# The modulation product of a two-layer diffusion block moved from TensorE to VectorE, all but its first four groups

## The chip, the cores and the metric

The kernel runs on 1 core of one Trainium2 chip. The metric is the device time of one execution in microseconds (us). The kernel before took 1662.61 us, the median of three runs (1662.46 to 1664.08). All times of rows come from one profiled execution of it, whose span is 1662.0 us.

## The reference, cut to what matters

Two layers (D_MODEL 1024) work on 256 tokens x and 256 tokens of context. Each has a mixer of three branches (spatial gating, differential attention, a gated delta rule) and a feed-forward with a convolution. Both are entered through a norm that is scaled and shifted by the modulation, and left through a gate by it. The modulation is one vector of 6144 numbers per layer for x and one for the context, each a product of a vector of 1024 with a matrix:

```
mod_x = silu(c) @ w_mod[l] + b_mod[l]            # [1, 6144]
mod_c = silu(c_ctx) @ w_mod[l] + b_mod[l]
sh1_x, sc1_x, gt1_x, sh2_x, sc2_x, gt2_x = split(mod_x, 6)
h_x = rms_norm(x, norm1_g[l]) * (1 + sc1_x) + sh1_x
y_x, y_c = hybrid_mixer(h_x, h_c, ...)           # the same for ctx
x = x + gt1_x * y_x
h_x = rms_norm(x, norm2_g[l]) * (1 + sc2_x) + sh2_x
x = x + gt2_x * conv_ffn(h_x, ...)               # silu(gate) * val, w_up, w_down
...
return x
```

The last layer goes on with x alone behind the mixer's inputs: of its modulation the context's half is needed for the first shift and scale only.

## The kernel before, in words

Activations lie with features on partitions and 512 tokens (256 of context, 256 of x) along the row; in the last layer 256 behind the mixer's keys. A projection goes by column tiles of 128 features. For each, SP loads the weights as f32, 512 KB (`wr`, three buffers, L266); ScalarE rounds them to a first part `wh` and VectorE subtracts for the rest `wl` (`split`, L262, four buffers each); TensorE multiplies wh by hh, wl by hh and wh by hl (`mm3`, L284), where hh and hl are the two parts of the activations. A column tile with 1024 inputs is 24 products of 512 columns.

The names of the rows: pqkv, pqk and ptm are projections of the mixer, psc the attention scores, pwo the output projection, pup and pdn the two projections of the feed-forward. In the delta rule sX, sL, sT, sLC and sLR belong to the triangular solve (`gdn_solve`, L1146), a chain of small VectorE operations sT, sL, sT, sL, ... on tiles of 32 x 32; U is its result, and the scan over chunks follows. axc, asq, qkss, qkrs and rsqt belong to the norm of attention's queries and keys.

A norm ends (`norm_end`, L522) with a chain: pss sums the squares, rsqv to rs is an inverse square root in small VectorE operations, pb spreads it over the partitions on TensorE, then xn, hh and hl are made, and the next projection starts with the first of them. TensorE has none of its big products to do meanwhile; three of these gaps bear on the change: ahead of the feed-forward of layer 0, ahead of layer 1, ahead of its feed-forward.

The modulation before (`mod_product`, L449) uses the conditioning as the stationary operand: per half group of 256 columns SP loads 1 MB of w_mod (`wm`), and 8 products of 128 x 32 by 256 columns add into `pmod`. A group (512 features, of 12 per layer) ends with `mod_finish` (L455): a VectorE transpose `m` of 128 x 512, four small products pmc, and one addition of the bias into `modv`. Groups go where the program calls `mod`: four of layer 0 at the start, six in its mixer behind the solve, the last two as filler in the gap ahead of the feed-forward, layer 1's first four inside layer 0's feed-forward, and the rest as filler in the gap ahead of layer 1, in its mixer and in its gap.

The order of the work is set by a list scheduler when the kernel is built: it takes the instructions of the program by priority and its own estimate of times and writes a fixed order for each engine; the delta rule is wrapped in `high_priority`. On the chip each engine then runs its list strictly in turn, SP's list of loads too: a load that waits for its buffer holds all loads behind it.

Of the kernel before, what the change touches and what calls it, by code (L numbers as in the profile page):

```python
# [10 lines left out]
F32 = mybir.dt.float32  # L11
# [16 lines left out]
FILL = (("p4", "p4"), ("t4a", "t4b"))  # L28
# [68 lines left out]
def host_layout(i):  # L97
# [7 lines left out]
    o["wmod"] = f(i["w_mod"].reshape(L, 8, 128, 12, 2, 256).transpose(0, 3, 4, 2, 1, 5))  # L105
# [67 lines left out]
class _Kernel:  # L173
# [97 lines left out]
    def wblock(self, src, n, step):  # L271
        """the two float32r parts of a block of weights [128, n], in pieces of `step` columns."""
# [16 lines left out]
    def proj_fm(self, src, kt, xh, xl, c0, ps):  # L289
        """ps[:, :NT-c0] = W^T x for one column tile of W laid out [128, kt*128]."""  # L290
# [5 lines left out]
    def first_load(self, srcs, i, j):  # L296
        """half i of the rows of column tiles j and j + 1, to be split by first_w."""
# [17 lines left out]
    def proj_first(self, srcs, xh, xl, c0, pss):  # L315
        """as proj_fm for several column tiles at once; goes along with h as its parts appear."""
# [21 lines left out]
    def run(self):  # L338
# [4 lines left out]
        for l in range(L):  # L343
# [3 lines left out]
            early = self.mod(1, (4, 5, 6), (5,), "g") if last else iter(())  # L347
            hh, hl = self.norm_end(N, steps(early, 2, 3, 2) if last else self.first)
            c0 = 256 if last else 0
            xf, N = self.mixer(l, hh, hl, xsrc, c0, early)  # L350
            late = self.mod(l, (10, 11), (), "g")
            hh, hl = self.norm_end(N, steps(late, 2, 3, 1))
            N = self.ffn(l, hh, hl, xf, c0, itertools.chain(late, self.mod(1, range(4), (9, 10)) if not last else ()))
# [11 lines left out]
    def start(self):  # L365
# [18 lines left out]
        for n, loads in enumerate((((0, 0), (0, 2)), ((0, 4),), ((1, 0), (1, 2)), ())):  # L384
            self.mod_ahead(0, order[2 * n:2 * n + 2], places[2 * n:2 * n + 2])
# [10 lines left out]
    def load_rest(self):  # L396
        """the constants and parameters that the first products do without."""
# [33 lines left out]
    def mod_load(self, l, g, h, where):  # L431
        """half of the columns of group g, [128, 8, 256], in a slot or in tiles of a part of its size."""
        src = self.a["wmod"][l, g, h]
        if isinstance(where, int):
# [31 lines left out]
    def mod(self, l, groups, places, tag="a"):  # L466
# [916 lines left out]
```

## Time and profile before

| | before |
|---|---|
| median of 3 runs | 1662.61 us |
| span of the profiled execution | 1662.0 us |
| TensorE busy | 1623.0 us, 98% |
| VectorE busy | 1084.7 us, 65% |
| ScalarE busy | 760.9 us, 46% |
| chain that ends last, through TensorE | 88% |

The profiled execution's own time is known as its span alone; it lies 0.6 us below the median. A busy share is an average over the span: a stage can be bound by an engine that is half idle in the whole. The chain names what released what, back from the last instruction. In a timeline row the bracket says how long the engine was idle before and on whom it waited. Matmuls overlap, so that their starts, not their durations, tell TensorE's pace.

### The profile page before, as it was taken

The numbers are of one execution on the slowest core, as the hardware profiler recorded it, in microseconds if no ns is written. First come the engines' busy times: TensorE is split into PE (matmuls) and PEld (weight loads), VectorE is DVE, ScalarE is ACT, GpSimd is POOL, SyncE is SP. The second block draws the span as 40 slices with busy tenths as digits, with TensorE's granted clock in tenths as the row PEclk, the third lists the DMA queues.
The fourth block names the chain that finished last, engine by engine and source line by source line (L and its number), as shares of the span: only waits on it lengthen the run. The fifth ranks groups of instructions, "written<-read, shape, count | busy, mean of one in ns | idle before, by whom it ended". The sixth has DMA issues, their size and how long they took to land.

```text
span 1662.0 us, 28498 instructions
## 1 busy us (share of the span) xinstructions
PE 1623.0 (98%) x11278; PEld 1355.4 (82%) x11278; DVE 1084.7 (65%) x2557; ACT 760.9 (46%) x1445; POOL 6.6 (0%) x16
## 2 busy tenths in 40 slices
PE   5999999999999999999999999999999999999999
PEld 3777887876788887778888887778878799999999
DVE  5658678666744456756446655658678775788685
ACT  3553622256532333534234442653722764566564
POOL 0000000000000000000000000000000000000000
PEclk9999899999999999999999999999999999999999
DMA  8553111421233444533333335441114356755665
GB/s 327 202 192 118 40 39 52 140 89 39 74 92 102 145 147 155 213 127 93 92 107 101 97 120 169 164 154 52 40 52 140 92 153 224 226 155 174 190 185 153
DMA packets 61254, 217.24 MB, mean 131 GB/s; under 512 B 7104, under 2 KB 13248, under 8 KB 55360
## 3 DMA queue, kind: packets, MB, share of 16 engines
q1 hardware_dynamic: 59248, 207.65, 39.3%
q10 hardware_dynamic: 1872, 7.77, 1.3%
q8 instruction: 88, 1.44, 0.4%
q14 instruction: 46, 0.38, 0.1%
HBM read 212.25 MB, written 3.15 MB: 130 GB/s over the span
## 4 chain that ended last, share of the span: by engine, by line
PE 88%; DVE 5%; ACT 2%; DMA 2%; issue 1%; SPq 0%; ACTq 0%; DVEq 0%
PE pup L239 22%; PE pg L239 11%; PE pdn L239 11%; PE pqkv L239 7%; PE ptm L239 7%; PE pbr L239 6%; PE pwo L239 3%; PE pmod L239 3%; PE pu L239 2%; PE psc L239 2%; PE pS L239 2%; PE pj L239 1%; ACT U L236 1%; PE pkS L239 1%; PE po L239 1%; PE pV L239 1%
## 5 line engine op out<-in xcount | busy, mean ns | idle before, releaser
L236 ACT ACTIVATE wh<-wr 128x512 fp32r<-128x512 f32 (+1 forms) x594 | 367.6, 622 | 441.8 <-PE pdn L239 108.5
L218 DVE TENSOR_TENSOR wl<-wr,wh 128x512 fp32r<-128x512 f32 (+1 forms) x592 | 400.1, 680 | 236.1 <-ACT wh L236 233.3
L239 PE MATMUL pup<-hh,wh 128*128 128x512 f32 (+1 forms) x704 | 237.9, 338 | 1.0 <-ACT hh L236 0.9
L239 PE MATMUL pup<-hh,wl 128*128 128x512 f32 (+1 forms) x704 | 236.8, 337 | 0.0
L239 PE MATMUL pup<-hl,wh 128*128 128x512 f32 (+1 forms) x704 | 236.2, 336 | 0.0
L233 DVE SCALAR_TENSOR_TENSOR fcv<-pup,par,fcv 128x510 f32<-128x510 f32 (+1 forms) x176 | 107.3, 611 | 81.4 <-ACT fcv L236 81.1
L239 PEld LDWEIGHTS pup<-hh,wh 128*128 128x128 f32 x704 | 133.6, 190 | 17.6 <-ACT fcv L236 2.5
L239 PEld LDWEIGHTS pup<-hl,wh 128*128 128x128 f32 x704 | 133.5, 190 | 14.0 <-DVE hl L233 0.2
L239 PEld LDWEIGHTS pup<-hh,wl 128*128 128x128 f32 x704 | 133.7, 190 | 13.6
L239 PE MATMUL ptm<-wh,hh 128*128 128x256 f32 x448 | 132.1, 295 | 0.0
L239 PE MATMUL ptm<-wh,hl 128*128 128x256 f32 x448 | 131.4, 294 | 0.0
L239 PE MATMUL pg<-hh,wl 128*128 128x512 f32 (+1 forms) x384 | 130.8, 341 | 0.0
L239 PE MATMUL pg<-hh,wh 128*128 128x512 f32 (+1 forms) x384 | 130.7, 340 | 0.1
L239 PE MATMUL ptm<-wl,hh 128*128 128x256 f32 x448 | 130.6, 292 | 0.0
L239 PE MATMUL pg<-hl,wh 128*128 128x512 f32 (+1 forms) x384 | 129.9, 338 | 0.0
L239 PE MATMUL pdn<-fh,wh 128*128 128x512 f32 (+1 forms) x352 | 118.5, 337 | 0.0
L239 PE MATMUL pdn<-fh,wl 128*128 128x512 f32 (+1 forms) x352 | 118.3, 336 | 0.0
L239 PE MATMUL pdn<-fl,wh 128*128 128x512 f32 (+1 forms) x352 | 118.0, 336 | 0.0
L236 ACT ACTIVATE fcv<-pup,par 128x512 f32<-128x512 f32 (+1 forms) x88 | 51.1, 581 | 91.1 <-PE pup L239 91.1
L239 PEld LDWEIGHTS ptm<-wh,hh 128*128 128x128 f32 x448 | 88.1, 197 | 4.7 <-issue 4.2
L239 PEld LDWEIGHTS ptm<-wh,hl 128*128 128x128 f32 x448 | 88.2, 197 | 3.3 <-issue 2.9
L239 PEld LDWEIGHTS ptm<-wl,hh 128*128 128x128 f32 x448 | 87.9, 196 | 2.8 <-issue 2.2
(326 smaller groups left out, 3121.9 us busy)
## 6 DMA issues: line engine op xcount, KB each, us to landing
wr<-in_wup_dram SPq DMA_DIRECT2D x80, 512.0 KB, 3.7
wm<-in_wmod_dram SPq DMA_DIRECT2D x39, 1024.0 KB, 7.6
wr<-in_wfm_dram SPq DMA_DIRECT2D x78, 512.0 KB, 3.6
wr<-in_wtm_dram SPq DMA_DIRECT2D x32, 512.0 KB, 3.7
wr<-in_wdn_dram SPq DMA_DIRECT2D x32, 512.0 KB, 3.6
wr<-in_wbr_dram SPq DMA_DIRECT2D x24, 512.0 KB, 3.6
wr<-in_wo_dram SPq DMA_DIRECT2D x16, 512.0 KB, 4.3
wm<-in_wmod_dram SPq DMA_DIRECT2D x14, 512.0 KB, 4.2
```

What stands on the lines that cost most here:

```text
L218: self.nc.vector.tensor_tensor(out=out, in0=a, in1=b, op=op)
L233: self.nc.vector.scalar_tensor_tensor(out=out, in0=a, scalar=s, in1=b, op0=op0, op1=op1)
L236: self.nc.scalar.activation(out, a, f, bias=bias, scale=scale, **k)
L239: self.nc.tensor.matmul(out, lhsT, rhs, start=start, stop=stop, **k)
```

## The change

Four groups of layer 0 stay as they are, at the start. The other 80 column tiles of 128 features (32 of layer 0, 48 of layer 1) come from a transposed copy of w_mod, `wmt`, with a tile's features on partitions and the 1024 inputs along the row. SP loads one such tile (512 KB, one buffer); VectorE multiplies it by silu of the conditioning (`scb`, the same on all partitions, loaded and passed through one ScalarE instruction at the start of the mixer) with one scalar_tensor_tensor whose accum_out is the sum along the row: a feature's product. The context takes one such instruction, its products written to `mj`, and x another, written over the tile. Layer 1's tiles from 16 on are done for x alone. After four tiles one addition adds the bias. The generator `mod` is advanced by `more`, one tile at a time, between column tiles of the projections of layer 0 (70 tiles in the text of the program; the last ten are asked for by `branch` in layer 1). The fillers in the gaps go. The bulk of the rest is deleted comments; gains and gates of the last layer are taken for x alone.

```
 def host_layout(i):
-    o["wmod"] = f(i["w_mod"].reshape(L, 8, 128, 12, 2, 256).transpose(0, 3, 4, 2, 1, 5))
+    o["wmod"] = f(i["w_mod"][0, :, :2048].reshape(8, 128, 4, 2, 256).transpose(2, 3, 1, 0, 4))
+    o["wmt"] = f(np.concatenate([i["w_mod"][0, :, 2048:], i["w_mod"][1]], 1).T.reshape(80, 128, 1024))
+    o["cB"] = f(np.broadcast_to(np.stack([i["c_ctx"], i["c"][0]], 0)[None], (128, 2, 1024)))
...
-            early = self.mod(1, (4, 5, 6), (5,), "g") if last else iter(())
-            hh, hl = self.norm_end(N, steps(early, 2, 3, 2) if last else self.first)
+            hh, hl = self.norm_end(N, iter(()) if last else self.first)
             c0 = 256 if last else 0
-            xf, N = self.mixer(l, hh, hl, xsrc, c0, early)
-            late = self.mod(l, (10, 11), (), "g")
-            hh, hl = self.norm_end(N, steps(late, 2, 3, 1))
-            N = self.ffn(l, hh, hl, xf, c0, itertools.chain(late, self.mod(1, range(4), (9, 10)) if not last else ()))
+            if not last:
+                self.mods = self.mod()
+            xf, N = self.mixer(l, hh, hl, xsrc, c0)
+            hh, hl = self.norm_end(N)
+            N = self.ffn(l, hh, hl, xf, c0)
...
-    def mod_load(self, l, g, h, where):
...
-    def mod(self, l, groups, places, tag="a"):
-        """modv[l] for groups of 4 column tiles, silu(cond) @ w_mod + b_mod; yields after each half of the columns,
-        which go through the next of `places` if they aren't there, and after each group."""
-        at = itertools.cycle(places)
-        for g in groups:
-            pm = None
-            for h in range(2):
-                r = self.wm.pop((g, h), None) or self.mod_load(l, g, h, next(at))
-                if pm is None:
-                    pm = self.bank(tag, "pmod")
-                self.mod_product(pm[:, 256 * h:256 * h + 256], r)
-                yield
-            self.mod_finish(l, pm, 4 * g, 4)
+    def mod(self):
+
+
+        nc = self.nc
+        sb = self.cp.tile([128, 2, 1024], F32, tag="scb", name="scb")
+        nc.sync.dma_start(out=sb, in_=self.a["cB"])
+        self.act(sb, sb, AF.Silu)
+        for n in range(80):
+            l, j = (0, 16 + n) if n < 32 else (1, n - 32)
+            vs = (0, 1) if l == 0 or j < 16 else (1,)
+            w = self.wp.tile([128, 1024], F32, tag="wm", name="wmt", bufs=1)
+            nc.sync.dma_start(out=w, in_=self.a["wmt"][n])
+            if n % 4 == 0:
+                m4 = self.small("m4", [128, 4, 2], bufs=2)
+            for v in vs:
+                o = w if v else self.tmp("mj", [128, 1024], BF16)
+                nc.vector.scalar_tensor_tensor(out=o, in0=w, scalar=1.0, in1=sb[:, v], op0=ALU.mult, op1=ALU.mult,
+                                               accum_out=m4[:, n % 4, v:v + 1])
+            if n % 4 == 3:
+                self.add(self.modv[l][:, j - 3:j + 1, vs[0]:], m4[:, :, vs[0]:],
+                         self.P(l, "bmod", j - 3, 4).unsqueeze(2).to_broadcast([128, 4, len(vs)]))
             yield
+
+    def more(self, n=1):
+        for _ in range(n):
+            next(self.mods, None)
...
-        for _ in itertools.chain(early, self.mod(l, range(4 + 3 * l, 10), ((5, 7, 8, 9), (5, 7, 8))[l])):
-            pass
...
-            if m == 1:
-                self.mod_ahead(l, ((10, 0), (10, 1), (11, 0), (11, 1)), (1, 8) + FILL)
...
 def branch(self, i, y, acc, final):      # behind each column tile of the gate
+            if l > 0 or i == 0 or i == 2 and m < 2:
+                self.more()
...
 def sgu(self):                           # and gdn_z; attn_project once per projection
+            self.more(l == 0)
...
 def ffn(self, l, hh, hl, xf, c0):
-                    next(mods, None)
+                if l == 0:
+                    self.more()
...
-                if m == 2 and hf == 1 and l + 1 < L:
-                    self.mod_ahead(l + 1, ((4, 0), (4, 1), (5, 0), (5, 1), (6, 0)), FILL + (("t4c", "gS"), ("tg",) * 4, ("go", "go", "go", "ta")))
+                if l == 0:
+                    self.more(1 + hf)
...
-            if hf == 0:
-                for _ in mods:
-                    pass
...
-    nc = bacc.Bacc("TRN2", target_bir_lowering=False, num_devices=1)
+    nc = bacc.Bacc("TRN2", target_bir_lowering=False, num_devices=1, dynamic_dma_scratch_size=1024)
```

The scheduler moves the new instructions: all 128 of VectorE stand before layer 1. The first place is VectorE in the solve of layer 0, between the sX transposes and sLR. Before:

```order
L218 TENSOR_TENSOR sT<-sX,sL 128x207
L218 TENSOR_TENSOR sL<-sL,sT 128x23x9
L218 TENSOR_TENSOR sT<-sX,sL 128x220
L218 TENSOR_TENSOR sL<-sL,sT 128x22x10
L218 TENSOR_TENSOR sT<-sX,sL 128x231
L218 TENSOR_TENSOR sL<-sL,sT 128x21x11
L218 TENSOR_TENSOR sT<-sX,sL 128x240
L218 TENSOR_TENSOR sL<-sL,sT 128x20x12
L218 TENSOR_TENSOR sT<-sX,sL 128x247
L218 TENSOR_TENSOR wl<-wr,wh 128x512
L218 TENSOR_TENSOR sL<-sL,sT 128x19x13
```

Now, at the same step of the chain (wmt and mj are the new products, m the sums, rsqt and qkrs the attention norm):

```order
L219 TENSOR_TENSOR wl<-wr,wh 128x512
L219 TENSOR_TENSOR sL<-sL,sT 128x22x10
L234 SCALAR_TENSOR_TENSOR qkrs<-rsqt,qkrs 128x8
L219 TENSOR_TENSOR wl<-wr,wh 128x512
L219 TENSOR_TENSOR sT<-sX,sL 128x231
L219 TENSOR_TENSOR axc<-axc,qkrs 128x512
L219 TENSOR_TENSOR sL<-sL,sT 128x21x11
L219 TENSOR_TENSOR sT<-sX,sL 128x240
L471 SCALAR_TENSOR_TENSOR mj,m_2038<-wmt,scb 128x1024
L219 TENSOR_TENSOR sL<-sL,sT 128x20x12
L471 SCALAR_TENSOR_TENSOR wmt,m_2038<-wmt,scb 128x1024
L219 TENSOR_TENSOR sT<-sX,sL 128x247
```

Two new products stand inside the chain sT, sL, and the attention projection's wl, axc and small operations have moved in among them; from the sX transposes to sLR VectorE has 116 instructions before and 178 now.

The second place is VectorE in the gap ahead of the feed-forward of layer 0, from the last sum of squares to xn. Before:

```order
L458 STREAM_TRANSPOSE m_6254<-pmod 128x512
L230 TENSOR_SCALAR rsqv<-pss 128x4
L230 TENSOR_SCALAR rs<-rsqv 128x4
L218 TENSOR_TENSOR rsqt<-rs 128x4
L218 TENSOR_TENSOR rsqt<-rsqt,rsqv 128x4
L233 SCALAR_TENSOR_TENSOR rsqt<-rsqt 128x4
L218 TENSOR_TENSOR modv_90<-pmc,part 128x8
L233 SCALAR_TENSOR_TENSOR rs<-rsqt,rs 128x4
L458 STREAM_TRANSPOSE m_6324<-pmod 128x512
L218 TENSOR_TENSOR rsqt<-rs 128x4
L233 SCALAR_TENSOR_TENSOR rsqt<-rsqt,rsqv 128x4
L218 TENSOR_TENSOR modv_90<-pmc,part 128x8
```

Now:

```order
L471 SCALAR_TENSOR_TENSOR mj,m_6385<-wmt,scb 128x1024
L231 TENSOR_SCALAR rsqv<-pss 128x4
L471 SCALAR_TENSOR_TENSOR wmt,m_6385<-wmt,scb 128x1024
L231 TENSOR_SCALAR rs<-rsqv 128x4
L219 TENSOR_TENSOR rsqt<-rs 128x4
L219 TENSOR_TENSOR rsqt<-rsqt,rsqv 128x4
L234 SCALAR_TENSOR_TENSOR rsqt<-rsqt 128x4
L234 SCALAR_TENSOR_TENSOR rs<-rsqt,rs 128x4
L219 TENSOR_TENSOR rsqt<-rs 128x4
L234 SCALAR_TENSOR_TENSOR rsqt<-rsqt,rsqv 128x4
L234 SCALAR_TENSOR_TENSOR rs<-rsqt,rs 128x4
```

Both transposes and both additions into modv are gone; one new product stands in front of rsqv and one between rsqv and rs.

The third place is SP's queue. Before, in layer 0, from the end of the first down projection through the second half of the feed-forward (x22) into the second down projection:

```order
L268 DMA wr<-in_wdn_dram 128x384
L268 DMA wr<-in_wup_dram 128x1024 x22
L268 DMA wr<-in_wdn_dram 128x1024
L268 DMA wr<-in_wdn_dram 128x384
L268 DMA wr<-in_wdn_dram 128x1024
L268 DMA wr<-in_wdn_dram 128x384
L268 DMA wr<-in_wdn_dram 128x1024
L442 DMA wm_8831<-in_wmod_dram 128x512
```

Now, where the second half of the feed-forward passes into its down projection:

```order
L466 DMA wmt<-in_wmt_dram 128x1024
L269 DMA wr<-in_wdn_dram 128x1024
L466 DMA wmt<-in_wmt_dram 128x1024
L269 DMA wr<-in_wdn_dram 128x384
L466 DMA wmt<-in_wmt_dram 128x1024
L269 DMA wr<-in_wdn_dram 128x1024
L466 DMA wmt<-in_wmt_dram 128x1024
L269 DMA wr<-in_wdn_dram 128x384
L466 DMA wmt<-in_wmt_dram 128x1024
```

Loads of wmt and of weights alternate, and since wmt has one buffer, each load of it waits for the new product of the tile before, and the wr behind it waits with it.

## Rows read from the trace of the kernel before

**Rows 1.** The page: busy us, share of the span, instructions.
```profile
PE 1623.0 (98%) x11278; PEld 1355.4 (82%) x11278; DVE 1084.7 (65%) x2557; ACT 760.9 (46%) x1445; POOL 6.6 (0%) x16
```

**Rows 2.** The page: shares of the chain that ended last, by engine.
```profile
PE 88%; DVE 5%; ACT 2%; DMA 2%; issue 1%; SPq 0%; ACTq 0%; DVEq 0%
```

**Rows 3.** Windows of tile pmod: stretch, its us, busy us and instructions by engine, PEclk.
```profile
60.00:150.00 90.00, 13.66 (x192) 5.99 (x192) 3.65 (x6) 1.00 0.50 182
654.00:664.00 10.00, 6.20 (x90) 2.89 (x90) 1.42 (x2) 1.00 0.79 305
664.00:744.00 80.00, 6.90 (x103) 2.75 (x102) 2.83 (x4) 1.00 0.52 178
1032.50:1042.50 10.00, 5.20 (x80) 2.51 (x80) 1.43 (x2) 1.00 0.90 301
1042.50:1140.00 97.50, 10.07 (x112) 3.73 (x112) 2.13 (x3) 0.98 0.38 122
1460.00:1467.30 7.30, 3.96 (x64) 1.94 (x64) 1.43 (x2) 1.00 0.50 146
```

**Rows 4.** Windows of all engines: stretch, its us, busy us by engine, PEclk.
```profile
112.00:150.00 38.00, 37.21 (x364) 22.64 (x363) 28.11 (x73) 17.16 (x31) 0.00 (x0) 1.00 0.37 140
150.00:187.00 37.00, 36.18 (x342) 35.42 (x341) 35.06 (x111) 14.67 (x23) 0.00 (x0) 1.00 0.30 90
187.00:210.00 23.00, 20.76 (x360) 19.42 (x355) 8.37 (x18) 18.61 (x28) 2.07 (x4) 0.78 0.01 2
...
700.00:744.00 44.00, 44.00 (x256) 32.98 (x256) 25.84 (x42) 16.74 (x28) 0.00 (x0) 1.00 0.40 133
1110.00:1115.00 5.00, 5.00 (x51) 3.19 (x51) 2.68 (x16) 1.80 (x3) 0.00 (x0) 0.72 0.87 283
```

**Rows 5.** Timeline of VectorE, layer 0's gap: start, us, operation, [idle before].
```profile
656.94 0.70 DVE L458 STREAM_TRANSPOSE m<-pmod 128x512 f32<-128x512 f32 x1
658.17 0.16 DVE L230 TENSOR_SCALAR rsqv<-pss 128x4 f32<-128x4 f32 x1 [0.52 <-PE pss L239]
...
659.26 0.17 DVE L218 TENSOR_TENSOR modv<-pmc,part 128x8 f32<-128x8 f32 x1
...
659.68 0.72 DVE L458 STREAM_TRANSPOSE m<-pmod 128x512 f32<-128x512 f32 x1 [0.18 <-PE pmod L239]
...
662.25 1.28 DVE L218 TENSOR_TENSOR xn<-xn,pb 128x512 f32<-128x512 f32 x2 [1.11 <-PE pb L239]
```

**Rows 6.** Timeline of TensorE, the same gap.
```profile
649.69 0.39 PE L239 MATMUL pwo<-yoh,wl 128*128 128x512 f32 x1
...
654.00 0.39 PE L239 MATMUL pwo<-yol,wh 128*128 128x512 f32 x1
...
663.98 0.50 PE L239 MATMUL pup<-hh,wh 128*128 128x512 f32 x1
```

**Rows 7.** Groups by form, VectorE: line, operation, shapes, count | busy us, mean ns.
```profile
L218 DVE TENSOR_TENSOR wl<-wr,wh 128x512 fp32r<-128x512 f32 x560 | 382.5, 687 | 202.1 <-ACT wh L236 199.4 <-PE ptm L239 0.2
...
L458 DVE STREAM_TRANSPOSE m<-pmod 128x512 f32<-128x512 f32 x20 | 14.2, 708 | 0.9 <-PE pmod L239 0.4 <-ACT vT L236 0.2
...
L233 DVE SCALAR_TENSOR_TENSOR pr<-pr,w 128x512 f32<-128x512 f32 x16 | 11.9, 746 | 0.2
...
L233 DVE SCALAR_TENSOR_TENSOR pr<-pr,w 128x256 f32<-128x256 f32 x8 | 3.8, 478 | 0.0
```

**Rows 8.** Chain of waits, 118 to 127 us: start, us, what.
```profile
119.23 6.17 DMA wm<-in_wmod_dram
```

**Rows 9.** Groups by form, ScalarE.
```profile
L236 ACT ACTIVATE sLt<-sL 128x1024 f32<-128x1024 f32 x2 | 4.1, 2028 | 4.1 <-DVE sL L218 4.1
```

**Rows 10.** DMA issues: count, KB each, median us from issue to landing.
```profile
wr<-in_wup_dram SPq DMA_DIRECT2D x80, 512.0 KB, 3.7
...
wm<-in_wmod_dram SPq DMA_DIRECT2D x14, 512.0 KB, 4.2
```

More of the change, by code (lines that the diff above doesn't have):

```diff
@@ L27 @@
 AHEAD = 300000
-FILL = (("p4", "p4"), ("t4a", "t4b"))
 PO = {}
@@ L384, in start @@
         for n, loads in enumerate((((0, 0), (0, 2)), ((0, 4),), ((1, 0), (1, 2)), ())):
-            self.mod_ahead(0, order[2 * n:2 * n + 2], places[2 * n:2 * n + 2])
+            self.mod_ahead(order[2 * n:2 * n + 2], places[2 * n:2 * n + 2])
             for i, j in loads:
@@ L429, in lam, with mod_ahead @@
         nc.vector.tensor_scalar_add(t, t, -li)
-    def mod_load(self, l, g, h, where):
-        src = self.a["wmod"][l, g, h]
-        if isinstance(where, int):
-            r = self.slot(where, "wm", [128, 8, 256])
-            self.nc.sync.dma_start(out=r, in_=src)
-            return [r[:, k] for k in range(8)]
-        r = []
-        n = 8 // len(where)
-        for i, tag in enumerate(where):
-            t = self.tp.tile([128, n, 256], F32, tag=tag, name="wm2", bufs={"p4": 2, "tg": 4, "go": 4, "ta": 3}.get(tag, 1))
-            self.nc.sync.dma_start(out=t, in_=src[:, n * i:n * i + n])
-            r += [t[:, k] for k in range(n)]
-        return r
-    def mod_ahead(self, l, which, places):
-        self.wm.update({w: self.mod_load(l, *w, p) for w, p in zip(which, places)})
+    def mod_ahead(self, which, places):
+        for (g, h), i in zip(which, places):
+            self.wm[g, h] = r = self.slot(i, "wm", [128, 8, 256])
+            self.nc.sync.dma_start(out=r, in_=self.a["wmod"][g, h])
     def mod_product(self, pm, r):
@@ L452, in mod_product @@
             q = k % 4
-            self.mm(pm[32 * q:32 * q + 32, :], self.sc[:, k, :], r[k], start=k < 4, stop=k >= 4)
+            self.mm(pm[32 * q:32 * q + 32, :], self.sc[:, k, :], r[:, k], start=k < 4, stop=k >= 4)
     def mod_finish(self, l, pm, j, n):
@@ L497, in norm_begin, with norm_gain @@
         if mods is None:
-            self.norm_gain(N, 0, 8)
+            self.norm_gain(N, 0, 8, c0 // 256)
         return N
-    def norm_gain(self, N, k0, k1):
-        g = self.P(N["l"], "n2g" if N["n"] else "n1g", k0, k1 - k0).unsqueeze(2).to_broadcast([128, k1 - k0, 2])
-        self.stt(N["a1"][:, k0:k1], self.modv[N["l"]][:, N["s"] + 8 + k0:N["s"] + 8 + k1, :], 1.0, g, ALU.add, ALU.mult)
+    def norm_gain(self, N, k0, k1, v=0):
+        g = self.P(N["l"], "n2g" if N["n"] else "n1g", k0, k1 - k0).unsqueeze(2).to_broadcast([128, k1 - k0, 2 - v])
+        self.stt(N["a1"][:, k0:k1, v:], self.modv[N["l"]][:, N["s"] + 8 + k0:N["s"] + 8 + k1, v:], 1.0, g, ALU.add,
+                 ALU.mult)
     @staticmethod
@@ L569, in norm_end, with mixer @@
         return hh, hl
-    def mixer(self, l, hh, hl, xsrc, c0, early):
+    def mixer(self, l, hh, hl, xsrc, c0):
         self.l, self.hh, self.hl, self.c0 = l, hh, hl, c0
@@ L614, in resid @@
             self._gt = (l, s), gt
-            self.nc.vector.tensor_scalar_mul(gt, self.modv[l][:, s:s + 8, :], scale)
+            v = c0 // 256
+            self.nc.vector.tensor_scalar_mul(gt[:, :, v:], self.modv[l][:, s:s + 8, v:], scale)
         gt = self._gt[1]
@@ L804, in attn_project @@
         for w in (2, 0, 3, 1, 4, 5):
+            self.more(l == 0)
             one(w)
@@ L1287, in gdn_z @@
             self.proj_fm(self.a["wfm"][l, 12 + m], 8, self.hh, self.hl, c0, p)
+            self.more(l == 0)
             self.flush()
@@ L1303, in gdn_out, with ffn @@
         return z
-    def ffn(self, l, hh, hl, xf, c0, mods):
+    def ffn(self, l, hh, hl, xf, c0):
         nc = self.nc
```

## The prediction, before the changed kernel was run

> **What bounds the kernel now.** I read the page first. TensorE is busy for 98% of the span and VectorE for 65% [rows 1]. The chain that ends last runs through TensorE for 88% and through VectorE for 5% [rows 2], so what this kernel gains must come out of TensorE's time, and VectorE seems to have room. It is an average, so I then asked by stages. The windows of the modulation product (pmod) show where the 640 products that the change removes lie: 13.66 us before 150, 6.20 in the gap between the last product of w_o and the first of the feed-forward, 6.90 inside the feed-forward, 5.20 in the gap ahead of layer 1, 10.07 in layer 1's mixer, 3.96 in its gap, together 46.0 us [rows 3]. The windows of all engines show the other side: from 150 to 187, the triangular solve of layer 0, VectorE is busy for 35.06 of 37 us; from 187 to 210 TensorE waits and its mean granted clock is 0.78; from 700 to 744 VectorE has 25.84 of 44 us [rows 4]. So the kernel is bound by TensorE except in the solve, where VectorE is as full, and in the three gaps, where a chain of small VectorE operations sets the end and pmod only fills [rows 5, 6].
>
> **The price of the new instruction.** No row of before sums along a row while it multiplies. The nearest ones take two f32 operands from SBUF: pr<-pr,w takes 746 ns for 512 columns and 478 for 256 [rows 7], so 268 ns per 256 columns, and 746 + 2 x 268 = 1.28 us for 1024. Against the plain wl subtraction of 687 the difference at 512 is 59 ns. From below I bound it by wl's rate without that, about 1.2 us; from above by twice the streaming part of 4 x 0.268 = 1.07, with 0.21 for the start: 2.35, should the sum need a second pass. I take 1.35, near the pr rows, with some 70 ns for writing the sum.
>
> [...]
>
> 128 of them (2 for each of 48 column tiles, 1 for each of 32) are 128 x 1.35 = 173 us of VectorE; 20 transposes of 708 ns [rows 7] go, 14 us. VectorE rises from 1085 to about 1244 us, 75% of the span. All of them stand before layer 1, so there it is not 75 but far more of the time.
>
> **Layer 0's mixer to the attention scores: 0 (-12 to +15).** TensorE loses 13.66 us of pmod, and the wait of 6.17 us on a load of wm ahead of the gates goes [rows 8], of which TensorE was idle for less than 1 us (37.21 busy of 38 [rows 4]). But the order of VectorE puts 4 new products between the decay and the sX transposes, and 5 between these and sLR; around them the scheduler pulls the attention projections forward, 17 wl instead of 12, 6 qkss sums instead of 2 and their small operations, 178 instructions instead of 116. At before's durations that stretch sums to 46 us before and 72 now, and it is the stretch that was already full (35.06 of 37 [rows 4]). So the solve ends some 22 to 25 us later. TensorE is given 9 more weight halves meanwhile, each 12 products of 0.227 us [rows 6] or 2.7 us, 24.5 in all, and has 13.66 fewer of pmod: it will be short of work by about 25 + 13.66 - 24.5 = 14 us, just what pmod's absence saved. Behind it the scan finds less left to run beside, but ends on the same number of weight halves at the first scores (68 in both). Net 0; the low end is nearly all of pmod gained, the high end the shortage without the gain. A Silu of 128 x 2048 on ScalarE (128 x 1024 took 2.03 us [rows 9]) stands ahead of kT's first; it is inside these bounds.
>
> **Attention core, branches, w_o: +2 (0 to +8).** Some 28 new instructions, 38 us, beside a TensorE that is full. VectorE was at about half here; a few wl will come late behind a product that waits for its load.
>
> **The gap before layer 0's feed-forward: +0.3.** In the chain rsqv to xn [rows 5] the transpose of 0.72, its wait of 0.18 and two additions of 0.17 go, 1.2 us; a product moves in front of rs (+1.35), and another in front of rsqv outlasts what it replaces by 0.1 or more.
>
> **Feed-forward of layer 0: -6.9 (-6.9 to 0), and +1.3 (0 to +11) for the loads.** The 6.90 us of pmod stand between full products [rows 3] and come out whole if VectorE keeps up. A pair of column tiles is 48 products or 10.88 us. VectorE was busy for 25.84 of 44 us, 6.4 per pair, and 30 products in 11 pairs add 2.7 x 1.3 = 3.5: 9.9 of 10.88, just enough. In the second half each column tile of 5.44 us has one product and one tile of weights, in a single buffer: product 1.35, the load behind it 3.7 [rows 10], 5.05 us together and below 5.44. But SP issues strictly in turn, so a late product holds the next wr. In the second down projection 12 tiles share 8 x 33 x 0.227 = 59.9 us, 4.99 each: 12 x 0.1 = +1.3. With the 4.2 us that the loads of wm took among others [rows 10] the loop takes 5.55: 22 x 0.11 + 12 x 0.56 + 2 for the first down projection = 11, the high end.
>
> **Layer 1: -1.1, -5 (-10 to 0), -0.7.** No new instruction stands there. In the gap ahead of it the transpose, its wait and the additions leave the chain, about 1.1 us as worked out above; in its second gap less, since there the chain was held by them only in part. Of the 10.07 us of pmod in the mixer's gates and solve [rows 3] I take half, since that stretch again ends on chains of VectorE and ScalarE.
>
> **The clock: +4.2 (0 to +10).** The three gaps held 1.00 with pmod as filler [rows 3]; without it TensorE does almost nothing there. Where it ran out of work, from 187 to 210, the granted clock fell, 0.78 in the mean; the small fall at 1110 to 1115 is 0.72 [rows 4], so 0.28 x 5 = 1.4 us at full speed lost. Three gaps: 4.2.
>
> [...]
>
> **The sum.** 0 + 2 + 0.3 - 6.9 + 1.3 - 1.1 - 5 - 0.7 + 4.2 = -5.9 us on the profiled span of 1662.0; the median of the runs is 0.6 above this span. Forecast 1656.7 us.
>
> **Rivals.**
> A. The sum along the row costs a second pass, 2.35 us. Then the first half of the feed-forward is VectorE's: 6.4 + 2.7 x 2.3 = 12.6 us a pair instead of 10.88, +19; the loop of product and load takes 6.05 in the second half, +13, and in the down projections +13 and (two products, 8.4 against 6.65) +16. The mixer's 48 take 48 us more, of which the 9 in keys and solve, 9 us, lie where VectorE is full. 1662 - 6 + 61 + 9 = about 1725. For it: nothing in the rows but that the sum is unseen; against it: 746 against 687. It decides from about 1.7 us per product.
> B. VectorE becomes the bound in layer 0's solve and the time doesn't come back: TensorE idles through the 25 us and the scan, with less to run beside it, keeps its length. 14 us without the gain, and the attention core's +8: 1657 + 15 + 6 = 1678. For it: 35.06 of 37; against it: VectorE's room after 187. It decides once the solve ends over 30 us later than now.
> C. The single buffer paces the feed-forward at 5.55 us a tile: 1657 + 10 = 1667.
> D. Full gain: 13.66 + 6.9 + 10.07 and the gaps' 2 come out of TensorE's 98% and the clock holds: about 1632. For it: the 98%; against it: the full solve [rows 4].
> E. The fill was free and the rest cancels: within 0.2% (3.3 us, about what a measurement of this kernel can tell from no change), 1662.
>
> **How the numbers follow.** Forecast 0.40, with its own range 1648 to 1662; D 0.14, A 0.10, B 0.16, C 0.12, E 0.08. Of the forecast's 0.40 some 0.33 lie below 1659.3 and 0.07 within 0.2%; C gives 0.03 to "same". Faster: 0.33 + 0.14 = 0.47, say 0.48. Same: 0.07 + 0.08 + 0.03 = 0.18, say 0.19. Slower: 0.33. The range leaves out A and the outer half of D: 1636 to 1690.
>
> **What would show it.** In the profile after: the new product's mean (1.3 to 1.4, or 2.3); VectorE's busy time about 1244; the sLR transposes some 22 us later, and the first scores at 343 all the same; no gap of TensorE from the first pup to the last pdn of layer 0, these 6 us nearer; the granted clock under 1 right after each gap; pdn blocks of the second half at 7.5 to 7.7 us. The forecast is wrong if the first scores come over 10 us from 343, or if SP's waits on the new product run into wr loads that TensorE waits for.

## The result, and the profile after

| | before | changed |
|---|---|---|
| median of 4 runs | 1663.34 us | 1648.30 us (1646.71 to 1651.85) |
| ratio | | 0.9904, 95% interval 0.9892 to 0.9916 |
| span of the profiled execution | 1662.0 us | 1645.3 us |
| TensorE busy | 1623.0 us, 98% | 1585.5 us, 96% |
| VectorE busy | 1084.7 us, 65% | 1201.7 us, 73% |

The change is 15 us faster (1.0% by the ratio in the table, 0.9% by the two medians); 6 were forecast, in a range of 1636 to 1690 us. The first rows of the page and of the chain of the changed kernel, to hold against [rows 1, 2]:

```profile
PE 1585.5 (96%) x10478; PEld 1339.4 (81%) x10478; DVE 1201.7 (73%) x2793; ACT 763.0 (46%) x1451; POOL 6.6 (0%) x16
...
PE 78%; DVE 9%; DMA 4%; ACT 4%; issue 3%; ACTq 0%; DVEq 0%
```

TensorE's share of the chain (the waits followed back from the last instruction) fell from 88% to 78%: the kernel is still TensorE's, with more waiting in it. The new instructions, by form (count | busy us, mean ns | idle time before, and what ended it):

```profile
L471 DVE SCALAR_TENSOR_TENSOR wmt<-wmt,scb 128x1024 f32<-128x1024 f32 x80 | 97.6, 1220 | 34.0 <-DMA wmt<-in_wmt_dram 33.6
...
L471 DVE SCALAR_TENSOR_TENSOR mj<-wmt,scb 128x1024 bf16<-128x1024 f32 x48 | 58.6, 1221 | 31.8 <-DMA wmt<-in_wmt_dram 31.8
...
L471 DVE DVE_READ_ACCUMULATOR wmt<-wmt,scb 128x1 f32 x80 | 6.6, 83 | 0.0
```

A product takes 1220 ns and a separate readout of the sum 83 ns, 1.30 us together against 1.35 in the sum of the prediction. The last column shows that VectorE stood idle for 66 us in front of products, nearly all of it waiting for their loads. With a second buffer in the feed-forward (e6 below) 27 us of it are left, so most of it goes with the single buffer.

Where the time went, by the starts of stages in the two traces, and in a second execution of the changed kernel (e5 below), so that a reader sees what two executions differ by:

| stage, TensorE's starts | before | changed | again | changed less before |
|---|---|---|---|---|
| start to pba, layer 0 | 112.2 | 114.9 | 117.5 | +2.7 |
| pba to the first scores | 228.9 | 217.5 | 218.8 | -11.4 |
| first scores to the last pwo | 312.9 | 312.5 | 312.5 | -0.4 |
| last pwo to the first hl product of pup | 10.6 | 12.2 | 12.2 | +1.7 |
| pup to the first fl product of pdn | 129.2 | 121.5 | 120.9 | -7.7 |
| pdn, second half, pdn | 238.7 | 241.2 | 241.3 | +2.5 |
| gap ahead of layer 1 | 10.8 | 12.0 | 11.2 | +1.2 |
| pqkv to pba, layer 1 | 60.5 | 62.5 | 62.4 | +2.0 |
| pba to the last pwo, layer 1 | 356.5 | 348.1 | 347.5 | -8.3 |
| gap ahead of its feed-forward | 7.8 | 8.4 | 8.4 | +0.6 |
| feed-forward to the last pdn | 190.1 | 190.8 | 191.2 | +0.7 |

(pba is the projection for the delta rule's gates and stands for the start of its part; the scores are psc; fl is the second part of the activations that pdn multiplies, as hl is for pup; a gap is counted up to the first hl product behind it. "pdn, second half, pdn" is the rest of the feed-forward, down to its last pdn.)

So the gain lies in three places, layer 0's delta rule, its feed-forward and layer 1's mixer, 27 us, and 11 are given back at the gaps and edges. The first of these places, in windows of the changed kernel (all engines: TensorE, its weight loads, VectorE, ScalarE, GpSimd, then the clock), against [rows 4]:

```profile
150.00:213.00 63.00, 61.73 (x593) 60.01 (x591) 62.11 (x196) 29.05 (x47) 0.00 (x0) 1.00 0.32 95
213.00:237.00 24.00, 21.37 (x309) 17.15 (x306) 14.86 (x41) 20.67 (x32) 2.07 (x4) 0.86 0.13 45
```

In 150 to 213, the solve, VectorE is busy for 62.11 of 63 us, as full as forecast. TensorE is busy for 61.73 of 63, which was not forecast: in the solve it was never short of work. It waits behind it (21.37 of 24 us, granted clock 0.86), as it did before (20.76 of 23, 0.78 in [rows 4]). The gaps, in TensorE's timeline ahead of the feed-forward of layer 0, against [rows 6] (start us, us, operation, and in brackets the idle time before and its releaser):

```profile
644.94 0.39 PE L240 MATMUL pwo<-yol,wh 128*128 128x512 f32 x1
648.02 1.05 PE L240 MATMUL pss<-cst,sqs 128*128 128x1 f32 x8 [2.69 <-DVE sqs L219]
651.92 2.08 PE L240 MATMUL pb<-cst,rs 128*128 128x128 f32 x8 [2.85 <-DVE rs L234]
655.72 0.79 PE L240 MATMUL pup<-hh,wh 128*128 128x512 f32 x1 [1.72 <-ACT hh L237]
656.31 0.63 PE L240 MATMUL pup<-hh,wl 128*128 128x512 f32 x1
656.74 0.63 PE L240 MATMUL pup<-hh,wh 128*128 128x512 f32 x1
```

The windows around it, with TensorE's clock third from the end:

```profile
650.00:655.00 5.00, 2.08 (x8) 1.78 (x8) 2.59 (x12) 0.24 (x1) 0.00 (x0) 0.55 0.39 126
655.00:660.00 5.00, 4.28 (x10) 3.41 (x11) 5.00 (x12) 3.17 (x8) 0.00 (x0) 0.50 0.00 0
```

Nothing stands between the last pwo and pss now. The clock is 0.50 to 0.55 from 650 to 660, pb takes 2.08 us, and the first products of pup come 0.43 us apart instead of 0.23. In VectorE's timeline of this gap the products stand as the order showed, against [rows 5]:

```profile
647.88 1.22 DVE L471 SCALAR_TENSOR_TENSOR mj<-wmt,scb 128x1024 bf16<-128x1024 f32 x1
649.03 0.08 DVE L471 DVE_READ_ACCUMULATOR mj<-wmt,scb 128x1 f32 x1
649.11 0.16 DVE L231 TENSOR_SCALAR rsqv<-pss 128x4 f32<-128x4 f32 x1
649.19 1.22 DVE L471 SCALAR_TENSOR_TENSOR wmt<-wmt,scb 128x1024 f32<-128x1024 f32 x1
...
650.33 0.17 DVE L231 TENSOR_SCALAR rs<-rsqv 128x4 int32<-128x4 int32 x1
...
654.04 1.28 DVE L219 TENSOR_TENSOR xn<-xn,pb 128x512 f32<-128x512 f32 x2 [2.17 <-PE pb L240]
```

In the feed-forward, the chain of waits of the changed kernel shows the only place where a load of wmt reaches TensorE, the end of the first half (fl is the row that the first down projection, pdn, waits for):

```profile
776.39 3.63 DMA wmt<-in_wmt_dram
...
780.05 1.25 DVE mj L471 x2
...
782.58 3.40 DMA wmt<-in_wmt_dram
...
787.23 0.62 DVE fl L219
...
787.89 52.88 PE pdn L240 x232
840.77 119.68 PE pup L240 x528
960.45 59.61 PE pdn L240 x263
```

Two loads, each behind the product before, hold fl (787.23), which the first down projection waits for. Behind it the second half (119.68 us for 528 products, 0.227 each) and the second down projection run without a wait.

### The profile page after: what moved, and what is told of

Same layout as the page of the kernel before. It is cut to its first block, busy times and chain, and to the rows that moved or that the text cites. A ratio compares the mean times of both kernels' runs of the same rounds, so it can differ in the third digit from the quotient of the medians.

```text
span 1645.3 us, 27181 instructions
## 1 busy us (share of the span) xinstructions
PE 1585.5 (96%) x10478; PEld 1339.4 (81%) x10478; DVE 1201.7 (73%) x2793; ACT 763.0 (46%) x1451; POOL 6.6 (0%) x16
## 4 chain that ended last, share of the span: by engine, by line
PE 78%; DVE 9%; DMA 4%; ACT 4%; issue 3%; ACTq 0%; DVEq 0%
PE pup L240 16%; PE pg L240 12%; PE pdn L240 11%; PE pqkv L240 8%; PE pbr L240 6%; PE pwo L240 4%; PE ptm L240 4%; DMA wmt<-in_wmt_dram 3%; PE pu L240 2%; PE psc L240 2%; PE pj L240 2%; PE pS L240 2%; ACT U L237 1%; PE pkS L240 1%; PE po L240 1%
## 5 line engine op out<-in xcount | busy, mean ns | idle before, releaser
L471 DVE SCALAR_TENSOR_TENSOR wmt<-wmt,scb 128x1024 f32<-128x1024 f32 x80 | 97.6, 1220 | 34.0 <-DMA wmt<-in_wmt_dram 33.6
L240 PEld LDWEIGHTS ptm<-wl,hh 128*128 128x128 f32 x448 | 86.7, 194 | 2.5 <-issue 1.7
```

The lines of the kernel that those rows point to most:

```text
L240: self.nc.tensor.matmul(out, lhsT, rhs, start=start, stop=stop, **k)
L471: nc.vector.scalar_tensor_tensor(out=o, in0=w, scalar=1.0, in1=sb[:, v], op0=ALU.mult, op1=ALU.mult, accum_out=m4[:, n % 4, v:v + 1])
```

## The experiments

All runs are measured against the kernel before on the same chip; every edit starts from the changed kernel. The stages' starts come from the traces.

**e1, e11: the three gaps filled again.** Products on constants, which nobody reads, go into the gaps as pmod did, 48 in each gap; the trace has two rows for each such product, so 96, not the 48 records of the expectation.

```
+    def warm(self, tag, *counts): ...   # 8 products 128x32 by 256 columns per count, into one bank
-            hh, hl = self.norm_end(N, iter(()) if last else self.first)
+            hh, hl = self.norm_end(N, self.warm("g", 2, 2, 2) if last else self.first)
...
-            hh, hl = self.norm_end(N)
+            hh, hl = self.norm_end(N, self.warm("g", 2, 2, 2))
```

> The changed kernel with products that nobody reads (128x32 by 256 columns on resident constants, 48 records in each) put back into the three gaps of the norms, nothing else. Theory 1, the clock: in the changed kernel's gap ahead of layer 1 pss takes 1.86 us for 1.05, pb 2.08 for 1.16, and the first 13 projections run at 0.43 us instead of 0.23, 2.6 us more, together 4.3 us; three such gaps give 10 to 13 us back: about 1636 us, granted clock 1.00 in and behind the gaps. Rival, the VectorE chain sets the gaps and the clock is only a sign: within 2 us of the changed kernel's 1648. Third, the filler stands in the way of pss and pb: slower than 1650.

Measured: 1642.81 us, ratio 0.9863 (0.9838 to 0.9888). The gap ahead of layer 1 in e1, in TensorE's timeline:

```profile
1020.45 2.78 PE L240 MATMUL pwarm<-cst,scond 128*32 128x256 f32 x42
1023.21 1.05 PE L240 MATMUL pss<-cst,sqs 128*128 128x1 f32 x8
1024.19 1.93 PE L240 MATMUL pwarm<-cst,scond 128*32 128x256 f32 x32
1026.11 1.16 PE L240 MATMUL pb<-cst,rs 128*128 128x128 f32 x8
1027.19 1.50 PE L240 MATMUL pwarm<-cst,scond 128*32 128x256 f32 x22
1028.98 0.50 PE L240 MATMUL pqkv<-hh,wh 128*128 128x512 f32 x1 [0.29 <-ACT hh L237]
```

The windows of e1 behind it, for the clock:

```profile
1025.00:1030.00 5.00, 4.71 (x58) 2.88 (x47) 3.58 (x12) 1.71 (x4) 0.00 (x0) 1.00 0.33 111
1030.00:1035.00 5.00, 5.00 (x23) 4.13 (x22) 5.00 (x11) 2.96 (x8) 0.00 (x0) 1.00 0.00 0
```

And the second of these windows in the changed kernel:

```profile
1030.00:1035.00 5.00, 4.52 (x11) 3.56 (x12) 5.00 (x12) 2.93 (x8) 0.00 (x0) 0.50 0.00 0
```

pss takes 1.05 again, pb 1.16, the clock stays at 1.00, and the last pdn to the first hl product of layer 1 takes 9.7 us for 12.0 (10.8 before the change). By the trace of e1 the three gaps and the products behind them give 3.0, 4.4 and 1.1 us, 8.5 together (6.9 in the trace of e11), so theory 1 holds for the place. The whole gained less. Beside the two others below, the same kernel was run again:

> The fill of three gaps once more, in more rounds, beside the two others: 1640 to 1644 us, 0.3 to 0.5% below the changed kernel; if its first result was one of a lucky set of executions, 1646 or more.

Measured: 1648.29 us, ratio 0.9901 (0.9886 to 0.9915). Over the eight runs of each, the median is 1644.9 us with the fill and 1648.1 without (its own four and e5's): 3 us, not 8. Even these 3 are near what the runs can tell, since the two results of one and the same filled kernel lie 5.5 us apart. Within its eight runs the time goes with the mean granted clock of the run: 0.986 in the three above 1648, 0.988 to 0.990 in the four from 1641 to 1645, 0.993 in the one at 1639.5. So what sets these eight executions apart shows in the clock.

The traces show where some of the 8 us is given back. Layer 1's mixer, from pba to the last pwo, takes 351.3 and 350.8 us in e1 and e11, for 348.1 in the changed kernel, and in these two traces the clock falls in the delta rule's gates. Windows of e11 in that stage:

```profile
1094.40:1114.20 19.80, 18.75 (x122) 15.77 (x120) 9.77 (x42) 10.01 (x21) 0.00 (x0) 0.90 0.28 78
```

The same stage in the changed kernel:

```profile
1094.40:1112.50 18.10, 17.06 (x121) 14.06 (x121) 9.57 (x39) 10.06 (x20) 0.00 (x0) 1.00 0.27 80
```

From pba to pU (the first products behind the solve) of layer 1 e1 and e11 take 82.7 us, the changed kernel 79.7: 3 us of 8 are lost there again. But the fill is not shown to be the cause. e6 below, which has no fill, takes 82.5 there, with the same fall:

```profile
1095.50:1115.30 19.80, 18.76 (x122) 15.77 (x120) 9.77 (x41) 10.13 (x21) 0.00 (x0) 0.90 0.28 78
```

And e2, which has the fill, takes 79.6, at a clock of 1.00, and loses time later in the mixer. Every trace with a fill has 350.0 to 351.3 us in the mixer of layer 1; without one it is 347.5 to 348.9 in four (the changed kernel, e3, e4, e5), 350.0 in e6 and 360.8 in e7.

**e2, e9: the gap around psq filled too.** There four halves of pmod stood before.

```
         self.act(e[32 * t0:], ssp[32 * t0:], AF.Copy)
+        w = self.warm("a", 2, 2, src=(self.qT_[:, 1, 256:512], e[:, 0:256])) if self.l == 0 and name == "rk" else iter(())   # e9: 3, 0
+        next(w, None)                                                          # and once more behind psq
         p = self.bank("b", "psq")
```

> As the fill of three gaps, and 32 more such records around psq in layer 0's mixer, where pmod stood before. Theory 1: in the changed kernel the clock is 0.50 to 0.59 from 85 to 95 us, and psq takes 1.79 us; another 2 to 4 us less than with three gaps, about 1633, and the first Xe back from 131.7 to about 128. Rival: pmod's removal there was a gain as it stands, so filling costs up to 2 us against three gaps.

Measured: 1644.03 us, ratio 0.9878 (0.9851 to 0.9905). It doesn't tell: the scheduler moved the conv steps cv behind the inverse square root, and TensorE waited 2.62 us for them. So the fill ahead of psq alone, with all else in the changed kernel's order:

> The fill of three gaps, and 24 more products ahead of psq in layer 0, where TensorE is idle for 2.6 us; the order of all other instructions is as in the changed kernel, which it was not in the fill of four gaps (there a projection waited 2.6 us on cv, so that run didn't tell). Theory 1: the clock at 85 to 95 us rises from 0.50 to near 1, 2 to 3 us less from psq to pba (31.1 before it), the whole 2 us below the fill of three gaps. Rival: the gap behind psq, still empty, lets the clock fall all the same: no gain, or up to 1 us lost, since the filler waits for qT and ends late.

Measured: 1644.77 us, ratio 0.9883 (0.9867 to 0.9898). Windows of e9, against 0.50 and 0.59 of the changed kernel at 85 and 90:

```profile
85.00:90.00 5.00, 3.15 (x53) 2.07 (x42) 2.47 (x9) 2.54 (x4) 0.00 (x0) 1.00 0.02 3
90.00:95.00 5.00, 5.00 (x23) 4.11 (x23) 2.48 (x6) 3.97 (x8) 0.00 (x0) 1.00 0.00 0
...
785.00:790.00 5.00, 3.99 (x9) 2.71 (x10) 4.75 (x9) 0.91 (x2) 0.00 (x0) 0.50 0.42 109
790.00:795.00 5.00, 5.00 (x21) 4.03 (x20) 1.89 (x4) 0.63 (x1) 0.00 (x0) 0.84 0.41 144
```

From psq to pba it takes 27.5 us for 31.1, 3.6 less, as theory 1 expected. Part of it only moved: the fill waits 1.48 us for qT, and psq starts later behind it. From the last projection product ahead of psq to pba it is 30.5 us before, 34.2 in the changed kernel and 32.1 in e9, so 2 us came back. The whole is no better than the fill of three gaps (1644.9), and the last two rows show one reason: at the start of the first down projection, where TensorE waits for fl, the clock now falls, where it stood at 1.00 in the changed kernel, and from there to the last pdn it takes 245.1 us for 241.2.

**e10: half the fill.** The counts are 1, 1, 1.

> The fill of three gaps with half the products, 24 in each and none behind pb, the order of all else as in the changed kernel. If any work in the gap holds the clock: as the fill of three gaps, 1640 to 1643. If the clock follows how much of the gap is filled: half of the gain or none, 1645 to 1648, with pb at 2.08 us and the first projections at 0.43 us apart.

Measured, in five runs: 1646.68 us, ratio 0.9898 (0.9882 to 0.9913). In the gap ahead of layer 1 pb takes 2.08 us and the clock is 0.59 behind 1025:

```profile
1025.00:1030.00 5.00, 2.44 (x9) 2.14 (x10) 2.69 (x9) 1.32 (x4) 0.00 (x0) 0.59 0.26 99
```

So in this trace half of the fill does not hold the clock to the end of the gap: pss keeps its 1.05 us, pb not its 1.16.

**e3: no product before the solve is done.**

```
+        hold = self.cp.tile([128, 1], F32, tag="hold", name="hold")
+        nc.vector.tensor_scalar_mul(hold, self.U_[:, 3, 1, 3, 63:64], 0.0)
-        self.act(sb, sb, AF.Silu)
+        self.act(sb, sb, AF.Silu, bias=hold)
...
-            U = self.gdn_solve(g)
+            U = self.U_ = self.gdn_solve(g)
```

> The changed kernel, but silu of the conditioning takes a zero computed from the last column of U, so that no new product can stand in the gates, keys and solve of layer 0; the scheduler then also leaves the attention projections behind (120 VectorE instructions from sX to sLR instead of 178). Theory 2, TensorE was fed through the longer solve and the time came back: sLR moves from about 208 back to 185 to 190 us, the first scores stay at 335 within 3, the whole within 3 us of 1648. Rival B, the delay of the solve is lost time: the first scores come 8 to 14 us earlier, the whole at 1634 to 1640. Third, the products now crowd the scan: slower, 1652 or more.

Measured: 1661.91 us, ratio 0.9990 (0.9979 to 1.0002): the third case. The solve is short again, pU at 193.4 for 213.1, but pj, the projection that follows the scan, first comes at 347.4 instead of 334.4 (the first scores of this order stand elsewhere, in the scan), and the last pwo 12.7 us later. The solve's 20 us were not lost time.

**e4: no products at all.** Their loads go too, and the sums are zero, so that the kernel leaves out most of the modulation.

```
-            w = self.wp.tile([128, 1024], F32, tag="wm", name="wmt", bufs=1)
-            nc.sync.dma_start(out=w, in_=self.a["wmt"][n])
-            for v in vs: ...
+                nc.vector.memset(m4, 0.0)
```

> The changed kernel without the 80 loads and the 128 new products; sums are zero instead, so the modulation of all but the first four groups is left out. It shows what the new work itself costs. Theory 2, it is nearly all hidden: 5 to 8 us less than 1648 (3 in layer 0's gates, 2.5 at the start of the first down projection, 0.5 in the gap), 1640 to 1643. Rival: VectorE and the queue of loads cost more in places that don't show as waits: 1632 or less.

Measured: 1647.39 us, ratio 0.9897 (0.9879 to 0.9916), the changed kernel's time. That is a sum of two things, since the scheduler set another order. From the last pwo of layer 0 to the end e4 takes 995.4 us, for 1000.4 and 998.6 in the two traces of the changed kernel: there the products and loads cost 3 to 5 us, of them 2.5 at the first down projection (238.7 for 241.2, as before the change). From pba to that last pwo it takes 534.3, for 530.0 and 531.2. So 128 products and 40 MB of loads cost a few us where they are placed, and the order that came with them gained about as much. In its order e4 is nearer to e3, and so e3 is best read against it, in the scan. Windows of e3 there:

```profile
222.00:260.00 38.00, 35.61 (x358) 27.95 (x358) 33.49 (x101) 5.35 (x9) 0.00 (x0) 1.00 0.24 76
260.00:300.00 40.00, 36.56 (x290) 25.63 (x291) 33.81 (x115) 7.50 (x11) 1.12 (x2) 0.91 0.13 44
```

The same stretch in e4, where VectorE (third) has less and TensorE (first) more:

```profile
222.00:260.00 38.00, 37.87 (x365) 30.54 (x363) 28.07 (x89) 8.79 (x15) 0.00 (x0) 1.00 0.10 29
260.00:300.00 40.00, 40.00 (x311) 27.26 (x310) 29.65 (x103) 7.88 (x12) 1.12 (x2) 1.00 0.12 41
```

And the two longest waits of TensorE in e3 from 222 to 300 us, on steps of the scan; in e4 no wait is listed there:

```profile
PE pkS L240 <- DVE gS L234: 1.9, 2, 1.0
PE pV L240 <- DVE rhs L234: 1.4, 1, 1.4
```

With 12 products in it TensorE is busy for 72.2 of 78 us, without them for 77.9: in the scan the products hurt. From pba to the first pj the four kernels take 230.6 us (before), 219.5 (changed), 232.1 (e3) and 223.1 (e4).

**e5: the changed kernel again.**

> The changed kernel as it is, beside the others on one chip. Expected: 1646 to 1652 us, as before; its trace shows how far stages that no edit touches differ from one execution to the next (the fill of three gaps left the order of all other instructions as it was, and yet its pba came 2.6 us later).

Measured: 1648.10 us, ratio 0.9894 (0.9865 to 0.9923). Its pba comes at 117.5 for 114.9, with no edit: in 25 to 30 and 35 to 40 us the granted clock is 0.68 and 0.66, in the other trace 0.91 and 1.00. 0.9 us of the 2.6 are there at the first pqkv, which starts at 23.9 for 22.9.

**e6, e8: a second buffer in the feed-forward.**

```
+            if n >= 24 and n % 2:
+                w = self.tp.tile([128, 1024], F32, tag="p4", name="wmt2", bufs=2)
```

> The changed kernel with a second buffer (the attention's, idle then) for every other tile of w_mod from the 25th on, that is in the feed-forward of layer 0 and just before. Theory 3, the single buffer costs only at the start of the first down projection, where a product that waits for its load holds fl: 2 to 3 us less than the changed kernel, the first down projection from 62.0 back to 59.7 us, the rest of the feed-forward unchanged at 5.44 us a column tile. Rival: the loop paces nothing, the 2.5 us stay in another form: 0.

Measured: 1647.34 us, ratio 0.9896 (0.9870 to 0.9921): no difference. Theory 3 holds for the place: TensorE's wait for fl is gone, and the first down projection takes 59.7 us, for 62.1 in the changed kernel. But the scheduler used the room in another way too. It put more products into the gap ahead of the feed-forward, where pb then waited 4.9 us for rs (2.9 in the changed kernel), and the gap grew from 12.2 to 15.4 us; the second half took 121.2 for 119.9. From the first hl product of pup to the last pdn the feed-forward fell by 0.4 to 0.9 us only (361.8 for 362.7 and 362.2). With the fill:

> The fill of three gaps and the two buffers together, as the version that should beat both kernels. If both are losses of their own they add: 5.5 and 2.5 us below the changed kernel, about 1640. If the clock's fall in the gap had been hiding the late loads, it is no better than the fill alone, 1643.

Measured: 1646.08 us, ratio 0.9881 (0.9851 to 0.9911): no better than the fill alone.

**e7: both halves everywhere.**

```
-            vs = (0, 1) if l == 0 or j < 16 else (1,)
+            vs = (0, 1)
```

> The changed kernel, but layer 1's tiles from 16 on are done for the context too: 160 products instead of 128, the 32 more in the second half of the feed-forward and the second down projection. Theory 4, product, load and order of SP make a loop: a tile then takes 2 x 1.30 + 3.65 = 6.25 us instead of 4.95, against 5.44 and 4.99 of TensorE's work: 21 x 0.8 + 12 x 1.25 = up to 32 us more, less some for weights loaded ahead: 1665 to 1680. Rival, VectorE's free time takes them (42 us more of work at 73% of the span): 1650 or less.

Measured: 1687.64 us, ratio 1.0138 (1.0113 to 1.0162), 39 us more than the changed kernel. The loop is real, but not where it was expected: the feed-forward keeps its pace, and the products left over at its end stand ahead of the last sums of squares (sqs), which pss waits for. VectorE's timeline of e7 behind the last pdn at 1021:

```profile
1029.53 1.23 DVE L471 SCALAR_TENSOR_TENSOR mj<-wmt,scb 128x1024 bf16<-128x1024 f32 x1 [2.68 <-DMA wmt<-in_wmt_dram]
...
1035.54 1.23 DVE L471 SCALAR_TENSOR_TENSOR mj<-wmt,scb 128x1024 bf16<-128x1024 f32 x1 [3.51 <-DMA wmt<-in_wmt_dram]
...
1036.69 0.69 DVE L219 TENSOR_TENSOR sqs<-sqs,sq 128x512 f32<-128x512 f32 x1
...
1042.15 1.23 DVE L471 SCALAR_TENSOR_TENSOR mj<-wmt,scb 128x1024 bf16<-128x1024 f32 x1 [3.42 <-DMA wmt<-in_wmt_dram]
```

The one long wait of TensorE in e7, in the view of its waits (us in total, times, longest):

```profile
PE pss L240 <- DVE sqs L219: 28.5, 1, 28.5
```

From one tile to the next it takes 6.0 to 6.6 us, near the 6.25 expected; 28.5 us are waited for there, 26 more than in the changed kernel (2.7), and the mixer of layer 1 takes 12.7 us more.

## Why the prediction was right, and where it was off

**Sign and range** were right; the size was off by 9 us, and that by one step, in layer 0's mixer. Outside of this mixer the terms add to -7.9 (0.3 - 6.9 + 1.3 - 1.1 - 5 - 0.7 + 4.2); the table gives -7.3 from the last pwo of layer 0 on. That these two agree so well is luck: the clock cost twice its term, and the two terms for pmod, in the feed-forward and in layer 1's mixer, gained some 6 us more than theirs (below). The mixer's terms were 0 + 2, and the trace gives -9.1 (-5.2 in the second execution).

**The step that was off** is "it will be short of work by about 25 + 13.66 - 24.5 = 14 us, just what pmod's absence saved". VectorE was full in the solve and sLR came 23.6 us later, both as forecast. But 8.1 of these had come before the sX transposes, and the stretch from the first sX to sLR grew by 15.5 us (41.8 to 57.3), not by the 26 of the durations (46 to 72 by the trace too). The prediction added up durations, and VectorE instructions that follow each other overlap in the trace: a product at 647.88 lasts 1.22, its readout starts at 649.03, 0.07 us before its end. In the stretch most neighbours overlap by 0.08 to 0.09 us. Where a step of the chain stands right behind the step whose result it needs, they don't; there the next starts 0.03 to 0.04 us after the end of the one before. Before, 26 pairs in the stretch are of this kind:

```profile
163.26 0.42 DVE L218 TENSOR_TENSOR sL<-sL,sT 128x252 f32<-128x252 f32 x1
163.72 0.43 DVE L218 TENSOR_TENSOR sT<-sX,sL 128x255 f32<-128x255 f32 x1
```

Now there is one, since other work stands between the steps, as in these rows of the changed kernel:

```profile
178.13 0.40 DVE L219 TENSOR_TENSOR sL<-sL,sT 128x240 f32<-128x240 f32 x1
178.45 1.22 DVE L471 SCALAR_TENSOR_TENSOR wmt<-wmt,scb 128x1024 f32<-128x1024 f32 x1
```

So before, 46 us of durations stand in 41.8, and after, 72 in 57.3. Some 3 us of the difference come from the 25 pairs at 0.11 us each (0.03 and 0.08, an estimate from these rows), the rest from there being more neighbours that overlap. And the 9 halves were counted up to sLR while the growth was counted from sX: 5 of them stand there, 13.6 us of products for 15.5. TensorE stayed busy (61.73 of 63). So all of pmod behind pba came out (-11.4 for 9.2 of pmod), and only the 4.46 us around psq didn't: there pmod had been free filler, and its going cost 3.7 (34.2 us for 30.5 from the last product ahead of psq to pba), of which 2.7 show at pba. The prediction had set as a sign of its failure that the first scores come over 10 us from 343. That was all but met: their row went from 341.1 to 332.4, and pj, which starts behind them, from 342.8 to 334.4 (336.3 and 338.3 in the second execution).

**The price of a product**: 1.30 for 1.35. With the sum an instruction takes 1220 ns for 1024 columns, where the prediction put the pr rows, without a sum, at 1.28 us for as many (an estimate from [rows 7]). Of its 1.35 the 70 ns for writing the sum stood in no row of before; the readout took 83. Rival A, which had 2.35, is out by that. VectorE's busy time rose by 117 us and not by 159. The sum of its durations rose by 155 (1209 to 1364 us in the two traces), so the new work was sized rightly; the page counts overlapped time once, and that is the 38 us between.

**The feed-forward**: -7.7 at the first half for -6.9 + 1.4 of clock; e1's trace, with the clock at 1.00, has 119.8 us there, 9.4 less than before. Of these 9.4, 6.9 are pmod's busy time and 1.0 is that of the small products pmc, which the term left out; the rest I can't put to a row. The loop cost 2.5 for 1.3, at the start of the first down projection and not in the second half, as e4 and e6 show; rival C's 5.55 us a tile didn't come, since the load landed in 3.6 (the page's median for wmt). SP's list ran in turn as stated: in the trace of the changed kernel each load of wmt behind the first is issued 0.03 us after the last readout of the tile before, and the load listed behind it 0.47 us later at the soonest.

**Layer 1**: -8.3 in the mixer and +2.0 in its first projections, -6.3 for the -5. The gap ahead of it lost the transposes and additions as worked out (1.1 us, which e1 shows at full clock: 9.7 for 10.8), but grew by 0.4 to 1.2 us, since pss took 1.86 us for 1.05 and pb 2.08 for 1.16, with the clock at 0.76 from 1020 to 1025 and 0.50 from 1025 to 1030.

**The clock**: 4.2 was forecast; e1 shows 8.5 in place. The gap ahead of layer 1 costs twice: inside it, where pss (1.86 for 1.05) and pb (2.08 for 1.16) take 0.8 and 0.9 us more, and behind it, where 13 products start 0.43 us apart for 0.23 (2.6 us). The 1.4 us a gap that the prediction took from [rows 4] were the price of one fall between full products, without the work inside a gap. But refilling wins about 3 us of the 8 by the runs. From 1025 to 1035, at the end of the gap ahead of layer 1 and behind it, the clock is 0.50 in the changed kernel, where the gap is empty, and 1.00 in e1, where it is filled; in e10, with half the fill, it is 0.59 from 1025 to 1030.

**Rival B** (the solve as the bound) is refuted in this placement: TensorE doesn't idle through the solve (61.73 us busy of 63), and in e4, whose solve is short (pU at 197.2) and which has no products, pj comes no earlier behind pba (223.1 us for 219.5). e3, at 1662, shows that products can hold TensorE one stage later, in the scan; B had 1678. **Rival D** was nearer than the forecast on the mixers (9.1 or 5.2 of its 13.66, 6.3 of its 10.07), and wrong on the gaps, where it let the clock hold; its terms add to 1630, not to the 1632 that it states. **Rival E**, no change, is out: the ratio's interval ends at 0.9916.

What stays open: why the clock falls in layer 1's gates in some traces, with the fill (0.90 in e11) and without it (0.90 in e6, 1.00 in the changed kernel), and so whether more than 3 us can be had. No version was clearly better than the fill of three gaps, 1644.9 over eight runs; e2 (1644.0) and e9 (1644.8) can't be told from it.

## What to carry to other kernels

In this kernel the work that filled TensorE's gaps was free only as long as it was there: without it the clock stood at 0.50 at the end of the gap ahead of layer 1, pss and pb took 0.8 and 0.9 us more in it, and the 13 products behind it 2.6. So before taking such work out, price the gap at the lower clock that the trace shows, inside and behind it. A gain that a trace shows in one place (8.5 us here) need not be the gain of the whole (3 us): the clock fell at other places too (0.90 in layer 1's gates in e6 and e11), and not in the same ones in every execution, so read the effect from many runs. When work goes to an engine with room, ask not how full it is on average but what its list holds at each place: here the products in the solve left TensorE busy for 61.73 of 63 us, since the scheduler had moved other work in for it, and the kernel was 14 us slower with more of them in the scan a little later. The durations of VectorE's rows didn't add up here (72 us of them stood in 57.3); take the busy time of a window instead. And independent work between the steps of the solve's chain cost less than its durations, since the steps lost some 0.11 us wherever they stood right behind each other.

## What was not expected of the hardware

VectorE's sum along the row is read out by an instruction of its own, 83 ns, that the kernel's text doesn't have. In the solve most neighbours on VectorE overlap by some 0.08 us, but a step of the chain that stands right behind the step whose result it needs starts 0.03 to 0.04 us after its end. And the same kernel reaches its first long stage 2.6 us apart in two executions (pba at 114.9 and 117.5), as much as several of the effects measured here: 0.9 us lie between them at the first projection already and 2.9 at psq (83.8 and 86.7), and the granted clock differs on the way (0.91 and 0.68 in 25 to 30 us, 1.00 and 0.66 in 35 to 40).
